# Rotary queries and keys computed feature-major, four heads' halves on the same partitions, and scores on four row tiles

## The chip, the cores and the metric

The kernel runs on one core of a Trainium2 chip. The metric is the device time of one launch in microseconds (us); less is better. TensorE (PE) multiplies matrices, its weight loads are shown apart (PEld); VectorE (DVE), ScalarE (ACT) and GpSimd (POOL) do the elementwise work; DMAs are issued from SyncE's queue (SP) and POOL's.

## The reference, cut to what matters

One layer of a decoder: an input projection, local attention beside a gated linear recurrence (HGRN2), cross-attention on 256 memory tokens, a gated feed-forward block. There are 256 tokens of 1024 features, all float32. The change lies in the attention's queries and keys:

```python
q_a, k_a, v_a, q_b, f_b, i_b, og_b, g_a, g_b = split_cols(xn @ w_in[l])   # q_a, k_a: (256, 1024), 16 heads of 64

def rope(t, pos):            # t: (1, 16 heads, 256 tokens, 64)
    ang = pos * inv_freq     # 32 angles a token, the same for all heads
    t1, t2 = t[..., :32], t[..., 32:]
    return concatenate([t1 * cos(ang) - t2 * sin(ang), t2 * cos(ang) + t1 * sin(ang)])

s = einsum('bhqd,bhkd->bhqk', rope(q), rope(k)) * 64 ** -0.5   # causal; softmax; times v
```

With 256 tokens the block attention is one causal block, so each head needs scores of 256 queries against up to 256 keys.

## The kernel before, in words

**Weights and precision.** Every weight matrix is streamed in units of 128 x 2048 floats (the list `ORDER`, laid out on the host by `lay`). `prep` turns a unit into two halves, `hi` (ACT, line 254, rounded) and `lo` (DVE, line 258, the remainder), each in two pieces of 128 x 1024. There are three buffers for each half, and `nxt` prepares two units ahead of the one in use. The activations are held as `Xh` and `Xl` in `XX`, and a product is the sum of three: hi by hi, hi by lo, lo by hi.

**Two forms of GEMM.** `gemm_t` keeps the tokens' features stationary and streams the weights: 128 tokens on the output's partitions, 512 output features along its columns; one call (two units, 512 features, 256 tokens) has 96 multiplications of 512 columns, in the three lines 310 to 312. `gemm_f` keeps the weights stationary and streams the tokens: 128 output features on the partitions, tokens along the columns; one call is one unit of 256 features and has, for each of two feature blocks, eight pairs: line 331 (the weights' `hi` against `Xh` and `Xl`, 512 columns) and line 332 (the weights' `lo` against `Xh`, 256 columns). The two halves of its 512 columns are added by `halves` (ACT copies one out, line 322, DVE adds the other, line 323). The HGRN2 queries (`ev_q`) and two projections of the cross-attention use `gemm_f` before; the attention's queries and keys use `gemm_t`.

**Queries and keys before.** `ev_rope` takes a block of 128 tokens by 512 features from PSUM: three DVE multiplications by the tables `Ct` and `St` (lines 877 to 879), one POOL addition (line 880), and two ticks later `turn`: four transposes on PE (line 885) and one ACT copy (line 886) into `qT` or `kT`, where the 64 features of a head lie on 64 partitions. There are eight such blocks.

**What sets PE's order.** PE's program order is the order of the code. Beside the GEMMs run generators; `tick`, called after each unit of weights, emits the next step of each. `hgrn` emits small multiplications (lines 642, 705, 715 and 723), `attention` the four quads of heads: `quad(j)` emits the scores of four heads (line 900, into four PSUM banks `as` of the pool `sm`, which has four), three ticks later the transposes of the probabilities (line 931), a tick after those the product with the values (line 945). The order on the other engines is made by the scheduler. A `MATMUL` row of line 900 before has a stationary operand of 64 partitions by 128 columns: two heads, on partitions 0 to 63 and 64 to 127, each in its own tile of rows of the array. An ordinary float32 multiplication (scores, values, lines 642 to 723) gives two MATMUL records in the trace, a transpose or a rounded product one.

Of the kernel before, what the change touches and what calls it, by code (L numbers as in the profile page):

```python
# [11 lines left out]
F32 = mybir.dt.float32  # L12
# [33 lines left out]
def plan():  # L46
    order = []

    def tgroup(name, base):
        return [("T", name, base + c * 512, kh) for c in range(2) for kh in range(2)]  # L50

    order += [("T", "w_in", 4096 + c * 512, kh) for kh in range(2) for c in range(2)]
    order += [("F", "w_in", 3 * 1024 + c * 256) for c in range(4)]
    for base in (5, 2, 0, 1, 6):
        order += tgroup("w_in", base * 1024)
    order += tgroup("w_in", 8 * 1024) + tgroup("w_in", 7 * 1024)
    order += tgroup("w_br_hgrn", 0) + tgroup("w_br_attn", 0)
# [59 lines left out]
def lay(ws):  # L117
    out = np.empty((len(ORDER), 128, 2048), np.float32)
    for i, u in enumerate(ORDER):
        if u[0] == "F":  # L120
            w = ws[u[1]][:, u[2]:u[2] + 256]
            out[i].reshape(128, 8, 256)[...] = w.reshape(8, 128, 256).transpose(1, 0, 2)
        elif u[0] == "T":
            w = ws[u[1]][u[3] * 512:(u[3] + 1) * 512, u[2]:u[2] + 512]
            if i < 3:
# [32 lines left out]
def bc(ap, n, axis):  # L158
    shape = list(ap.shape)
    shape.insert(axis, n)  # L160
    return ap.unsqueeze(axis).to_broadcast(shape)


def build(tc, A, out):
    nc = tc.nc
    V, SC, G, PE, SY = nc.vector, nc.scalar, nc.gpsimd, nc.tensor, nc.sync
    with ExitStack() as ctx:
# [29 lines left out]
        def bank(name, shape=(128, 512)):  # L197
            return sm.tile(list(shape), F32, name=name, tag="sm")
# [233 lines left out]
            part_x(k)  # L432


        Ct = cp.tile([128, 2, 64], F32, name="Ct")
        St = cp.tile([128, 2, 64], F32, name="St")

        def rope_tables():
            posf = small("posf", [2])
# [43 lines left out]
            tc.keep_in_program_order(SC.activation(m, r, AF.Sin))  # L483
            tc.keep_in_program_order(SC.activation(mh, t, AF.Sin))
            for i in range(2):
                rs = r_x[:, i:i + 1]
                for c in range(2):
                    G.tensor_scalar(Ct[:, i, c * 32:(c + 1) * 32], mh[:, i], rs, None, op0=ALU.mult)
                G.tensor_scalar(St[:, i, 0:32], m[:, i], rs, -1.0, op0=ALU.mult, op1=ALU.mult)
                G.tensor_scalar(St[:, i, 32:64], m[:, i], rs, None, op0=ALU.mult)  # L490

        rt = rope_tables()
        region = tc.manual_schedule(engines={mybir.EngineType.Pool})
# [372 lines left out]


        qx = big("B6", "qx", (128, 3072))
        qT = qx[:, 0:2048].rearrange("p (a b) -> p a b", a=8)
        kT = big("B11", "kT")  # L870

        def ev_rope(dst, c):
            def ev(t, ps):
                a = t2("ra")
                b = t2b("rb_")
                p3, a3, b3 = (z.rearrange("p (h d) -> p h d", d=64) for z in (ps, a, b))
                V.tensor_tensor(a3, p3, bc(Ct[:, t], 8, 1), op=ALU.mult)
                V.tensor_tensor(b3[:, :, 0:32], p3[:, :, 32:64], bc(St[:, t, 0:32], 8, 1), op=ALU.mult)
                V.tensor_tensor(b3[:, :, 32:64], p3[:, :, 0:32], bc(St[:, t, 32:64], 8, 1), op=ALU.mult)
                G.tensor_tensor(a, a, b, op=ALU.add)  # L880

                def turn():
# [7 lines left out]
        for c in range(2):  # L890
            gemm_t(X, ev_rope(qT, c))
        rows = (slice(0, 64), slice(64, 128))

        def quad(j):
            sc = []
            for hp in (2 * j, 2 * j + 1):
                ss = [bank("as", (128, 384)) for _ in range(2)]
                for q, o in ((slice(0, 128), slice(0, 128)), (slice(128, 256), slice(128, 384))):
                    for r, ps in zip(rows, ss):
                        PE.matmul(ps[:, o], qT[r, hp, q], kT[r, hp, 0:q.stop], start=True, stop=True)  # L900
                sc.append(ss)
            parts = ((0, 128), (128, 384))
            pr = []
            for ss in sc:
# [55 lines left out]
        oah = big("B12", "oah", dt=F32R)  # L960
        oal = big("B10", "oal", dt=F32R)
        ag = attention()
        gemm_t(X, ev_rope(kT, 0))
        start(ag)
        gemm_t(X, ev_rope(kT, 1))

        def ev_og(c):
            def ev(t, ps):
# [744 lines left out]
```

## Time and profile before

| | before |
|---|---|
| median of 3 runs (lowest, highest) | 593.89 us (593.01, 594.14) |
| profiled execution: its time, its span | 593.53 us, 591.4 us |
| PE busy | 584.3 us, 99% of the span |
| DVE, ACT, POOL busy | 448.0, 388.8, 119.5 us |
| granted TensorE clock, mean | 0.998 |

The span runs from the first to the last instruction of the program; the time has 2.1 us around it. Matrix instructions are pipelined, so a row's duration is longer than what it adds to PE's time; what it adds is read from the start of one piece to the start of the next.

### The profile page before, as it was taken

The numbers are of one execution on the slowest core, as the hardware profiler recorded it, in microseconds if no ns is written. First come the engines' busy times: TensorE is split into PE (matmuls) and PEld (weight loads), VectorE is DVE, ScalarE is ACT, GpSimd is POOL, SyncE is SP. The second block draws the span as 40 slices with busy tenths as digits, with TensorE's granted clock in tenths as the row PEclk, the third lists the DMA queues.
The fourth block names the chain that finished last, engine by engine and source line by source line (L and its number), as shares of the span: only waits on it lengthen the run. The fifth ranks groups of instructions, "written<-read, shape, count | busy, mean of one in ns | idle before, by whom it ended". The sixth has DMA issues, their size and how long they took to land.

```text
span 591.4 us, 8803 instructions
## 1 busy us (share of the span) xinstructions
PE 584.3 (99%) x3374; PEld 487.7 (82%) x3374; DVE 448.0 (76%) x630; ACT 388.8 (66%) x629; POOL 119.5 (20%) x135
## 2 busy tenths in 40 slices
PE   9999999999999999999999999999999999999995
PEld 7888888888888888888888888888888888888884
DVE  6598967778747784748968785987888887777943
ACT  7795645454767575658548677776858676776743
POOL 2897300222301530003202332200000000000002
PEclk9999999999999999999999999999999999999999
DMA  9877987489999899989986895666979969797601
GB/s 339 345 284 273 285 339 284 157 274 311 310 293 377 265 267 286 322 363 304 325 284 173 262 311 180 170 244 240 377 275 303 402 184 424 199 404 203 237 0 71
DMA packets 22585, 161.90 MB, mean 274 GB/s; under 512 B 2832, under 2 KB 3472, under 8 KB 5392
## 3 DMA queue, kind: packets, MB, share of 16 engines
q1 hardware_dynamic: 18368, 135.35, 58.1%
q0 software_dynamic: 3456, 25.17, 22.1%
q10 hardware_dynamic: 720, 0.84, 0.4%
q8 instruction: 26, 0.43, 0.3%
q14 instruction: 15, 0.12, 0.1%
HBM read 160.29 MB, written 34.60 MB: 330 GB/s over the span
## 4 chain that ended last, share of the span: by engine, by line
PE 99%; DVE 0%; ACT 0%; DVEq 0%; issue 0%; ACTq 0%
PE pst L310 13%; PE pst L312 12%; PE pst L311 12%; PE pqA L1129 11%; PE psf L331 8%; PE pqF L1129 6%; PE psf L332 4%; PE acc L310 3%; PE acc L312 3%; PE acc L311 3%; PE pqB L1129 3%; PE psg L588 1%; PE pso L311 1%; PE pso L310 1%; PE pso L312 1%; PE as L900 1%
## 5 line engine op out<-in xcount | busy, mean ns | idle before, releaser
L258 DVE TENSOR_TENSOR lo<-raw,hi 128x1024 fp32r<-128x1024 f32 (+1 forms) x126 | 158.1, 1274 | 48.9 <-ACT hi L254 48.5
L254 ACT ACTIVATE hi<-raw 128x1024 fp32r<-128x1024 f32 (+1 forms) x126 | 126.2, 1027 | 68.0 <-PE pst L312 37.6
L310 PE MATMUL pst<-hi,XX 128*128 128x512 f32 x224 | 89.0, 398 | 0.0
L312 PE MATMUL pst<-hi,XX 128*128 128x512 f32 x224 | 87.3, 390 | 0.0
L311 PE MATMUL pst<-lo,XX 128*128 128x512 f32 x224 | 87.3, 390 | 0.0
L310 PEld LDWEIGHTS pst<-hi,XX 128*128 128x128 f32 x224 | 42.1, 188 | 9.2 <-issue 0.7
L312 PEld LDWEIGHTS pst<-hi,XX 128*128 128x128 f32 x224 | 42.1, 188 | 9.0
L311 PEld LDWEIGHTS pst<-lo,XX 128*128 128x128 f32 x224 | 42.1, 188 | 8.2
L1368 DVE TENSOR_TENSOR lo<-raw,hi 128x2048 fp32r<-128x2048 f32 (+1 forms) x19 | 37.0, 1951 | 10.6 <-ACT hi L1360 10.5
L1360 ACT ACTIVATE hi<-raw 128x1024 fp32r<-128x1024 f32 x32 | 32.0, 1051 | 7.3 <-PE acc L312 5.3
L1368 DVE TENSOR_TENSOR lo<-rawx,hi 128x2048 fp32r<-128x2048 f32 x12 | 27.5, 2288 | 7.5 <-ACT hi L1360 7.5
L1399 POOL DMA_DIRECT2D b<-t x4 | 3.5, 885 | 123.4 <-DVE fu L1462 88.2
L1360 ACT ACTIVATE hi<-rawx 128x1024 fp32r<-128x1024 f32 x24 | 24.1, 1051 | 4.7 <-DMA rawx<-w 1.7
L1129 PE MATMUL pqA<-hi,SS 128*128 128x512 f32 x80 | 26.4, 391 | 0.0
L310 PE MATMUL acc<-hi,hids 128*128 128x512 f32 x62 | 24.4, 394 | 0.0
L312 PE MATMUL acc<-hi,hids 128*128 128x512 f32 x62 | 24.2, 390 | 0.0
L311 PE MATMUL acc<-lo,hids 128*128 128x512 f32 x62 | 24.1, 389 | 0.0
L331 PE MATMUL psf<-XX,hi 128*128 128x512 f32 x64 | 22.9, 401 | 0.0
L331 PE MATMUL psf<-H,hi 128*128 128x512 f32 x64 | 22.8, 400 | 0.0
L331 PE MATMUL psf<-M,hi 128*128 128x512 f32 x64 | 22.7, 398 | 0.0
L1368 DVE TENSOR_TENSOR lo<-b,hi 128x2048 fp32r<-128x2048 f32 x7 | 16.0, 2290 | 5.9 <-ACT hi L1360 5.9
L1368 DVE TENSOR_TENSOR px<-raw,px 128x2048 fp32r<-128x2048 f32 x8 | 18.3, 2284 | 2.1 <-ACT px L1360 2.1
(471 smaller groups left out, 1486.4 us busy)
## 6 DMA issues: line engine op xcount, KB each, us to landing
raw<-w SPq DMA_DIRECT2D x74, 1024.0 KB, 7.6
t<-w POOLq DMA_DIRECT2D x16, 1024.0 KB, 13.0
raw<-t SPq DMA_DIRECT2D x12, 1024.0 KB, 7.4
rawx<-w SPq DMA_DIRECT2D x10, 1024.0 KB, 7.9
b<-w SPq DMA_DIRECT2D x6, 1024.0 KB, 8.4
b<-w POOLq DMA_DIRECT2D x4, 1024.0 KB, 8.5
rawx<-t SPq DMA_DIRECT2D x4, 1024.0 KB, 6.9
b<-t POOLq DMA_DIRECT2D x4, 1024.0 KB, 8.6
```

What stands on the lines that cost most here:

```text
L254: SC.activation(hi[:, a], raw[:, a], AF.Copy)
L258: V.tensor_tensor(lo[:, a], raw[:, a], hi[:, a].bitcast(F32), op=ALU.subtract)
L310: PE.matmul(ps, xh, h, start=first, stop=False)
L311: PE.matmul(ps, xh, l, start=False, stop=False)
L312: PE.matmul(ps, xl, h, start=False, stop=last)
L331: PE.matmul(ps, w[0][:, k, a], X2[:, :, k], start=k == 0, stop=False)
L332: PE.matmul(ps[:, 0], w[1][:, k, a], X2[:, 0, k], start=False, stop=k == 7)
L588: PE.matmul(pss[c][t], z[:, k, t * 128:(t + 1) * 128], ws[c][0][:, k], start=z is Xh and k == 0, stop=False)
L900: PE.matmul(ps[:, o], qT[r, hp, q], kT[r, hp, 0:q.stop], start=True, stop=True)
L1129: PE.matmul(ps, x[k], z[:, k], start=first and k == 0 and i == 0, stop=k == 3 and i == 2, skip_group_check=not first)
L1360: pin(SC.activation(hi[:, a], raw[:, a], AF.Copy))
L1368: pin(V.tensor_tensor(lo[:, a], raw[:, a], hi[:, a].bitcast(F32), op=ALU.subtract))
```

## The change

The queries' and keys' projections go from `gemm_t` to `gemm_f`. Their weight units are laid out so that one unit of 256 features holds the lower 32 features of four heads in its first 128 columns and the upper 32 of the same four in its last 128 (the kind "R"). So a call leaves two blocks of 128 x 256 tokens, the lower and the upper halves of four heads on the same partitions, 32 a head, and the rotation works between the two blocks on equal partitions. It is DVE's two multiplications of 128 x 512 (by cosines, by sines) and POOL's two of 128 x 256, which write `qT` and `kT` directly; the transposes of `turn` and their copies are gone. The tables are made as `CS` (each token's 32 cosines and sines four times over, 128 wide) and turned once by four transposes (`angles`) into `turnsF`, in a buffer (B12) that the attention's output takes later. The scores of four heads now come from four tiles of 32 rows, one for each head, in two accumulating steps (lower and upper half) into the same four banks.

```diff
-    for base in (5, 2, 0, 1, 6):
+    for base in (5, 2):
         order += tgroup("w_in", base * 1024)
+    order += [("R", "w_in", base * 1024 + c * 256) for base in (0, 1) for c in range(4)]
+    order += tgroup("w_in", 6 * 1024)
...
+        elif u[0] == "R":
+            w = ws[u[1]][:, u[2]:u[2] + 256].reshape(8, 128, 4, 2, HD // 2).transpose(1, 0, 3, 2, 4)
+            out[i].reshape(128, 8, 256)[...] = w.reshape(128, 8, 256)
...
-        def ev_rope(dst, c):
-            def ev(t, ps):
-                a = t2("ra")
-                b = t2b("rb_")
-                p3, a3, b3 = (z.rearrange("p (h d) -> p h d", d=64) for z in (ps, a, b))
-                V.tensor_tensor(a3, p3, bc(Ct[:, t], 8, 1), op=ALU.mult)
-                V.tensor_tensor(b3[:, :, 0:32], p3[:, :, 32:64], bc(St[:, t, 0:32], 8, 1), op=ALU.mult)
-                V.tensor_tensor(b3[:, :, 32:64], p3[:, :, 0:32], bc(St[:, t, 32:64], 8, 1), op=ALU.mult)
-                G.tensor_tensor(a, a, b, op=ALU.add)
-
-                def turn():
-                    bk = bank("rT", (128, 4, 128))
-                    for j in range(4):
-                        PE.transpose(bk[:, j], a[:, j * 128:(j + 1) * 128], ident)
-                    SC.activation(dst[:, 4 * c:4 * c + 4, t * 128:(t + 1) * 128], bk, AF.Copy)
-                later.append(lambda: later.append(turn))
+        def angles():
+            b = bank("cs", (128, 2, 2, 128))
+            for c in range(2):
+                for i in range(2):
+                    PE.transpose(b[:, c, i], CS[:, c, i].rearrange("p n f -> p (n f)"), ident)
+            SC.activation(turnsF, b.rearrange("p c i t -> p c (i t)"), AF.Copy)
+
+        def ev_rope(dst, j):
+            z = t2("rz", (128, 2, 256))
+
+            def ev(m, ps):
+                halves(z[:, m], ps)
+                if m == 0:
+                    return
+                a, b = t2("ra", (128, 2, 256)), t2b("rb_", (128, 2, 256))
+                V.tensor_tensor(a, z, bc(turnsF[:, 0], 2, 1), op=ALU.mult)
+                V.tensor_tensor(b, z, bc(turnsF[:, 1], 2, 1), op=ALU.mult)
+                G.tensor_tensor(dst[:, j, 0], a[:, 0], b[:, 1], op=ALU.subtract)
+                G.tensor_tensor(dst[:, j, 1], a[:, 1], b[:, 0], op=ALU.add)
             return ev
...
-            for hp in (2 * j, 2 * j + 1):
-                ss = [bank("as", (128, 384)) for _ in range(2)]
-                for q, o in ((slice(0, 128), slice(0, 128)), (slice(128, 256), slice(128, 384))):
-                    for r, ps in zip(rows, ss):
-                        PE.matmul(ps[:, o], qT[r, hp, q], kT[r, hp, 0:q.stop], start=True, stop=True)
+            ss = [bank("as", (128, 384)) for _ in range(4)]
+            for q, o in ((slice(0, 128), slice(0, 128)), (slice(128, 256), slice(128, 384))):
+                for w in range(2):
+                    for r, ps in zip(quads, ss):
+                        PE.matmul(ps[:, o], qT[r, j, w, q], kT[r, j, w, 0:q.stop], start=w == 0, stop=w == 1)
```

Three places show what moves. On PE, in the queries' projection, the rows around one group of transposes (`rT`, two blocks of four) that stands before HGRN2's products `lv`; first before, then the same place of the change (line numbers are shifted by a few).

```order
L311 MATMUL pst<-lo,XX 128x512
L312 MATMUL pst<-hi,XX 128x512
L885 MATMUL rT<-cst,ra 128x128 x8
L705 MATMUL lv<-QK 32x32 x32
L310 MATMUL pst<-hi,XX 128x512
L311 MATMUL pst<-lo,XX 128x512
```

```order
L336 MATMUL psf<-XX,hi 128x512
L337 MATMUL psf<-XX,lo 128x256
L708 MATMUL lv<-QK 32x32 x32
L336 MATMUL psf<-XX,hi 128x512
L337 MATMUL psf<-XX,lo 128x256
```

The eight transposes are gone, and so are three other groups of eight; the products around them are pairs of 512 and 256 columns in place of triples of 512. On PE at the end of the keys' projection, the first quad's scores, before and after:

```order
L311 MATMUL pst<-lo,XX 128x512
L312 MATMUL pst<-hi,XX 128x512
L900 MATMUL as<-kT,qx 128x128 x2
L900 MATMUL as<-kT,qx 128x256 x2
L900 MATMUL as<-kT,qx 128x128 x2
L900 MATMUL as<-kT,qx 128x256 x2
L310 MATMUL pst<-hi,XX 128x512
```

```order
L336 MATMUL psf<-XX,hi 128x512
L337 MATMUL psf<-XX,lo 128x256
L907 MATMUL as<-kT,qx 128x128 x8
L907 MATMUL as<-kT,qx 128x256 x8
L315 MATMUL pst<-hi,XX 128x512
```

Eight multiplications become sixteen, of the same sizes, each with half the rows. On DVE at the start of the queries' projection, before and after (`lo` is the weights' remainder, QK and ATS belong to HGRN2):

```order
L258 TENSOR_TENSOR lo<-raw,hi 128x1024
L693 COPY_PREDICATED ATS<-lm,lp 128x8x16
L662 TENSOR_TENSOR QK<-QK,Tt 128x128x8
L693 COPY_PREDICATED ATS<-lm,lp 128x8x16
L877 TENSOR_TENSOR ra<-pst,Ct 128x512
L878 TENSOR_TENSOR rb__1267<-pst,St 128x8x32
L879 TENSOR_TENSOR rb__1267<-pst,St 128x8x32
```

```order
L263 TENSOR_TENSOR lo<-raw,hi 128x1024
L328 TENSOR_TENSOR rz<-psf,ku 128x256
L263 TENSOR_TENSOR lo<-raw,hi 128x1024
L328 TENSOR_TENSOR rz<-psf,ku 128x256
L696 COPY_PREDICATED ATS<-lm,lp 128x8x2x8
L890 TENSOR_TENSOR ra<-rz,tables 128x512
L891 TENSOR_TENSOR rb__1227<-rz,tables 128x512
L696 COPY_PREDICATED ATS<-lm,lp 128x8x16
```

The two additions `rz` (which wait for PE's blocks) now stand between the pieces of `lo`, and the multiplications read SBUF in place of PSUM.

## Rows read from the trace of the kernel before

**Rows 1.** The page: span, busy time of the engines, the chain by engine.

```profile
span 591.4 us, 8803 instructions
PE 584.3 (99%) x3374; PEld 487.7 (82%) x3374; DVE 448.0 (76%) x630; ACT 388.8 (66%) x629; POOL 119.5 (20%) x135
...
PE 99%; DVE 0%; ACT 0%; DVEq 0%; issue 0%; ACTq 0%
```

**Rows 2.** All waits of PE: who waited for whom, us, times, longest.

```profile
PE warm L404 <- PEq L1704: 0.8, 1, 0.8
```

**Rows 3.** Timeline of PE around transposes: start us, us, instruction, tiles, shape.

```profile
117.02 0.39 PE L312 MATMUL pst<-hi,XX 128*128 128x512 f32 x1
117.25 1.03 PE L885 MATMUL rT<-cst,ra 128*128 128x128 f32 x8
118.04 0.48 PE L310 MATMUL pst<-hi,XX 128*128 128x512 f32 x1
118.35 0.40 PE L311 MATMUL pst<-lo,XX 128*128 128x512 f32 x1
...
129.02 1.03 PE L885 MATMUL rT<-cst,ra 128*128 128x128 f32 x8
129.99 0.76 PE L705 MATMUL lv<-QK 128*32 128x32 f32 x64
...
157.39 1.95 PE L723 MATMUL lv<-QK 128*128 128x128 f32 x16
159.10 0.48 PE L310 MATMUL pst<-hi,XX 128*128 128x512 f32 x1
```

**Rows 4.** The same: ends of a run of `gemm_f`, of `gemm_t`, four transposes between.

```profile
34.79 0.48 PE L331 MATMUL psf<-XX,hi 128*128 128x512 f32 x1
...
51.82 0.40 PE L310 MATMUL pst<-hi,XX 128*128 128x512 f32 x1
...
239.32 0.66 PE L792 MATMUL hT<-cst,ATS 128*128 128x128 f32 x4
239.73 0.48 PE L310 MATMUL pst<-hi,ob 128*128 128x512 f32 x1
...
256.16 1.47 PE L931 MATMUL aT<-cst,ap 128*128 128x128 f32 x12
```

**Rows 5.** The same: the first quad's scores, and HGRN2's products on column tiles.

```profile
149.12 0.39 PE L312 MATMUL pst<-hi,XX 128*128 128x512 f32 x1
149.44 1.58 PE L900 MATMUL as<-kT,qx 64*128 64x128 f32 x16
150.95 0.50 PE L310 MATMUL pst<-hi,XX 128*128 128x512 f32 x1
...
98.94 0.89 PE L642 MATMUL lp<-QQ,QK 128*32 128x48 f32 x64
99.75 0.50 PE L310 MATMUL pst<-hi,XX 128*128 128x512 f32 x1
```

**Rows 6.** Busy time of the engines in stretches (PE, PEld, DVE, ACT, POOL).

```profile
28.26:51.82 23.56, 23.56 (x139) 20.58 (x138) 21.48 (x30) 19.79 (x37) 21.49 (x29) 1.00 0.73 269
99.75:149.44 49.69, 49.69 (x385) 40.84 (x377) 38.34 (x49) 23.30 (x31) 13.07 (x9) 1.00 0.80 270
```

**Rows 7.** Instructions of single lines: duration ns min/median/max, first and last start.

```profile
L323 DVE TENSOR_TENSOR kx<-psf,ku x16: 402/418/425, 316.2 to 376.9; 128x256 f32<-128x256 f32 x16
L322 ACT ACTIVATE ku<-psf x24: 357/366/390, 34.0 to 375.6; 128x256 f32<-128x256 f32 x24
L670 DVE TENSOR_TENSOR QK<-QK,Tt x1: 684/684/684, 144.1 to 144.1; 128x512 f32<-128x512 f32 x1
L877 DVE TENSOR_TENSOR ra<-pst,Ct x8: 682/691/692, 110.6 to 149.5; 128x512 f32<-128x512 f32 x8
```

**Rows 8.** DVE from 99.75 to 149.44 us, `lo` alone: count, busy us, mean ns.

```profile
L258 DVE TENSOR_TENSOR lo<-raw,hi 128x1024 fp32r<-128x1024 f32 x16 | 22.6, 1426 | 8.5 <-ACT hi L254 8.5
```

**Rows 9.** Timeline of DVE: the last piece of a weight unit's `lo`.

```profile
107.96 1.22 DVE L258 TENSOR_TENSOR lo<-raw,hi 128x1024 fp32r<-128x1024 f32 x1
```

More of the change, by code (lines that the diff above doesn't have):

```diff
@@ L432, in build @@
             part_x(k)
-        Ct = cp.tile([128, 2, 64], F32, name="Ct")
-        St = cp.tile([128, 2, 64], F32, name="St")
+        tables = big("B12", "tables", (128, 1024))
+        CS = tables[:, 0:512].rearrange("p (c i n f) -> p c i n f", c=2, i=2, n=4)
+        turnsF = tables[:, 512:1024].rearrange("p (c t) -> p c t", c=2)
         def rope_tables():
@@ L485, in rope_tables @@
             for i in range(2):
[L486 to L490, printed above, removed]
+                for c, z in enumerate((mh, m)):
+                    G.tensor_scalar(CS[:, c, i], bc(z[:, i], 4, 1), r_x[:, i:i + 1], None, op0=ALU.mult)
         rt = rope_tables()
@@ L868, in build @@
         qx = big("B6", "qx", (128, 3072))
-        qT = qx[:, 0:2048].rearrange("p (a b) -> p a b", a=8)
-        kT = big("B11", "kT")
-        def ev_rope(dst, c):
-            def ev(t, ps):
-                a = t2("ra")
-                b = t2b("rb_")
-                p3, a3, b3 = (z.rearrange("p (h d) -> p h d", d=64) for z in (ps, a, b))
-                V.tensor_tensor(a3, p3, bc(Ct[:, t], 8, 1), op=ALU.mult)
-                V.tensor_tensor(b3[:, :, 0:32], p3[:, :, 32:64], bc(St[:, t, 0:32], 8, 1), op=ALU.mult)
-                V.tensor_tensor(b3[:, :, 32:64], p3[:, :, 0:32], bc(St[:, t, 32:64], 8, 1), op=ALU.mult)
-                G.tensor_tensor(a, a, b, op=ALU.add)
-                def turn():
-                    bk = bank("rT", (128, 4, 128))
-                    for j in range(4):
-                        PE.transpose(bk[:, j], a[:, j * 128:(j + 1) * 128], ident)
-                    SC.activation(dst[:, 4 * c:4 * c + 4, t * 128:(t + 1) * 128], bk, AF.Copy)
-                later.append(lambda: later.append(turn))
-            return ev
@@ L890, in build @@
-        for c in range(2):
-            gemm_t(X, ev_rope(qT, c))
+        qT = qx[:, 0:2048].rearrange("p (j w t) -> p j w t", j=4, w=2)
+        kT = big("B11", "kT", (128, 4, 2, 256))
+        def angles():
[4 more added lines that the diff above has]
+            SC.activation(turnsF, b.rearrange("p c i t -> p c (i t)"), AF.Copy)
@@ L892, in build @@
+        angles()
+        for c in range(4):
+            gemm_f(XX, ev_rope(qT, c))
         rows = (slice(0, 64), slice(64, 128))
         def quad(j):
-            sc = []
-            for hp in (2 * j, 2 * j + 1):
-                ss = [bank("as", (128, 384)) for _ in range(2)]
-                for q, o in ((slice(0, 128), slice(0, 128)), (slice(128, 256), slice(128, 384))):
-                    for r, ps in zip(rows, ss):
-                        PE.matmul(ps[:, o], qT[r, hp, q], kT[r, hp, 0:q.stop], start=True, stop=True)
-                sc.append(ss)
+            ss = [bank("as", (128, 384)) for _ in range(4)]
[3 more added lines that the diff above has]
+                        PE.matmul(ps[:, o], qT[r, j, w, q], kT[r, j, w, 0:q.stop], start=w == 0, stop=w == 1)
+            sc = (ss[0:2], ss[2:4])
@@ L962, in build @@
         ag = attention()
-        gemm_t(X, ev_rope(kT, 0))
-        start(ag)
-        gemm_t(X, ev_rope(kT, 1))
+        for c in range(4):
+            if c == 2:
+                start(ag)
+            gemm_f(XX, ev_rope(kT, c))
         def ev_og(c):
```

## The prediction

> **What bounds the kernel now.** I read the page first: PE is busy for 99% of the span and the chain that ended last lies on PE for 99% of it [rows 1]. A busy PE need not be a limit, since it may be waiting inside its rows, so the waits come next: over the whole span PE waits once, 0.8 us before the warm-up [rows 2]. So the time is the length of PE's stream plus a short head and tail. What a change adds to or takes from that stream it adds to or takes from the time, as long as the other engines keep feeding it; and work taken from DVE, ACT or POOL alone is worth nothing. I therefore price the change in PE's timeline, always from the start of one piece to the start of the next, because the durations of pipelined rows overlap.
>
> **Transposes removed.** A group of eight goes from 117.25 to 118.04, 0.79 us, and the product behind it needs 0.31 us to its successor (118.04 to 118.35) where two products in a steady run lie 0.23 us apart (117.02 to 117.25): 0.87 us in all [rows 3]. Before HGRN2's column tiles the group takes 0.97 us (129.02 to 129.99), but then about 0.09 us of it is the change of tiles, which stays: a change to tiles without transposes takes 0.32 us from the last product (149.12 to 149.44) where 0.23 is normal [rows 3, 5]. That is 0.88. There are four such groups, two to each projection: 4 x 0.88 = **-3.5 us**.
>
> **Transposes added.** `angles` has four, once. Four transposes take 0.41 us (239.32 to 239.73) [rows 4], and the restart behind them 0.08 as above: **+0.5 us**. They need `CS`, which POOL makes where it made `Ct` and `St`, by four instructions in place of eight, some 40 us before; nobody waits for it.
>
> **The GEMM in its other form.** Both stream the same columns: 96 x 512 a call of `gemm_t`, twice a projection, against 64 pairs of 512 + 256. The rows tell what the shape costs. From 34.79 to 51.82 lie 48 pairs: 17.03 us, 0.3548 a pair. From 239.73 to 256.16 lie 72 products of 512 columns: 16.43 us, 0.2282 each, both runs with their restart [rows 4]. Two projections are 128 pairs, 45.4 us, in place of 192 products, 43.8 us: **+1.6 us**. So the projection itself gets dearer, since each weight block is loaded for 768 columns in two instructions, the second of them short; only the transposes pay for it.
>
> **Scores.** Before, a quad has 16 records (8 multiplications, two records each) and takes 1.51 us (149.44 to 150.95) [rows 5]. Its records stand for 8 x 128 + 8 x 256 = 3072 columns. A float32 record of 128 x 128 without tiles costs 1.71 / 16 = 0.107 us (157.39 to 159.10) [rows 3], so these 3072 columns one after another would cost 24 x 0.107 = 2.6 us; the two tiles of 64 rows run side by side. After, a quad has 32 records and 6144 columns, half the rows in each: 5.1 us if one after another, 2.6 us if two run side by side, 1.3 us if four do. Nothing here shows four row tiles. The nearest row is the one with four column tiles: 64 records of 48 columns in 0.81 us (98.94 to 99.75), 0.0127 each, where one alone would need 48/128 x 0.107 = 0.040 [rows 5]; more than three run side by side, with the start and the end counted in. I take four: a quad stays at 1.51 us, **0**. The bounds: nothing lower, since the columns divided by the tiles stay the same, and above, two at a time, 2.6 in place of 1.3 us in four quads, +5.2 us.
>
> A rule of the Trainium skill speaks against the scores: "TensorE: Matmul & The Clock Gate", section LDWEIGHTS, says that a load's time depends on its columns and not on its rows, so a load of 32 rows is as long as one of 64, and there are twice as many. By the rule alone, with two loads at a time, the sum would be that of the third rival below; the same page (Part 3, The mechanism) lets loads overlap where their row groups differ, which by itself gives my zero. No run here shows four.
>
> **Sum.** -3.5 + 0.5 + 1.6 + 0 = **-1.4 us**. The profiled execution took 593.53 us, so 592.1; the median before is 593.89, 0.36 above it, which makes **592.5 us** for the median, 0.24% less.
>
> **What must stay hidden.** DVE. A block of 256 features by 256 tokens (a unit of weights, some 5.6 us of PE) cost it 0.69 + 2 x 0.42 = 1.5 us; now it is two additions `rz` of 0.42 and two products of 0.68 (the row of 128 x 512 in SBUF), 2.2 us [rows 7]. Over eight units that is +5.5 us. In the stretch of the projections DVE is busy for 38.3 of 49.7 us; it becomes 43.8 of some 48.2, 91% [rows 6]. That this can be fed is shown by the HGRN2 queries, the same `gemm_f` with a heavier eviction: DVE is busy 21.5 of 23.6 us there, 91%, POOL 91% and ACT 84% as well, and PE waits nowhere [rows 2, 6]. ACT loses eight copies of the turned blocks and gets sixteen of 0.37 us [rows 7], far from full. What queues behind the new waits: `rz` waits for PE's block and the copy `ku`, and stands between the two pieces of `lo` on DVE's queue, as `ku` stands between the pieces of `hi` on ACT's. A `lo` that ended at 109.2 us belongs to a unit that PE starts at 118.04, 8.9 us later [rows 3, 9]. The second piece now moves behind the second block's eviction, half a unit or 2.8 us later; 6 us of cover remain. If the cover went, PE would wait on line 332 or 331 for `lo`.
>
> PSUM: the four score banks are the whole pool `sm`; before, the same four were taken in two steps within 1.5 us. The bank that `angles` takes is one more turn of the pool, beside work that is long read.
>
> **The rivals.**
> 1. *Two row tiles at a time.* For it: the trace shows two and no more for rows. Against it: four column tiles. Price +5.2 us, so -1.4 + 5.2 = +3.8: 597.7 us. It is the one on the other side; it turns the sign as soon as a quad's scores take more than 1.51 + 1.4/4 = 1.86 us.
> 2. *DVE falls behind.* For it: `lo` already takes 1.43 us on average against 1.22 alone (16 of them, 22.6 us, so 3.1 us of stretching beside POOL's additions) [rows 8, 9], and the two products now read SBUF only, as POOL does. If the stretching doubles, DVE has 47 of 48 us to do, and the order on its queue makes PE wait at some units; I price it at 2 us, between nothing and the 5.5 us that DVE gets in all. Then +0.6: 594.5 us.
> 3. *Loads of weights bound the scores.* With two of them side by side, 32 loads in 16 steps of 0.107 us are 1.7 us, in place of 1.3: +0.4 a quad, +1.6 in all. Then +0.2: 594.1 us. Against it: 16 loads of 64 rows are not seen to limit anything now.
> 4. *More is gained.* The restarts around the groups may be worth more than I see, or the pairs may run without the 0.1 us of their restart: -2.5, 591.4 us.
>
> **Chances.** Forecast (-0.9 to -2.0 us): 62%. Rival 1: 10%, rival 2: 12%, rival 3: 10%, rival 4: 6%. A measurement of this kernel tells some 0.2%, 1.2 us, from no change; my -1.4 lies close to that. Of the forecast's 62% I count two thirds, 41%, as faster and 21% as the same; rival 4 is faster; rival 3 the same; rival 2 half the same, half slower; rival 1 slower. Faster 0.47, same 0.36, slower 0.17. The range: up to 595.5 it holds the forecast and rivals 2 and 3, and leaves out rival 1 (10%) and the worst of rival 2; down to 591.5 it leaves out most of rival 4. The forecast's own range is 591.9 to 593.0.
>
> **What would show it.** In the profile of the changed kernel: no `rT`; four `cs` transposes in 0.4 to 0.5 us; 128 pairs at 0.353 to 0.357 us, so 45.2 to 45.7 us for both projections without the small work between; each quad's scores, 32 records, in 1.5 to 1.6 us, with groups of four starting some nanoseconds apart (right), or over 2.5 us (rival 1), or 1.8 to 2.0 (rival 3); no wait of PE on DVE or ACT between 100 and 160 us (rival 2 would show waits at the first product of a unit or at a `lo`). DVE should be busy about 43 us in that stretch. The prediction is wrong above all if the row tiles do not run four abreast, or if `lo` comes late.

## The result, and the profile after

The changed kernel takes **597.1 us** (median of 4 runs, 596.8 to 598.45) where the kernel before takes 593.5 beside it: a ratio of 1.0065, 95% interval 1.0045 to 1.0085. It is slower by 0.65%, 3.6 us; the forecast was 1.4 us faster, and 597.1 lies above the range. The profiled execution took 596.83 us, 3.3 more than the one before. One execution of `e_late` (831.6 us, mean clock 0.663) is left out below.

The page of the changed kernel, its span, its busy time and its chain by engine, answering to [rows 1]:

```profile
span 594.7 us, 9030 instructions
PE 585.1 (98%) x3474; PEld 489.7 (82%) x3474; DVE 453.4 (76%) x638; ACT 390.2 (66%) x638; POOL 121.2 (20%) x139
...
PE 84%; DVE 5%; DMA 4%; ACT 2%; issue 2%; POOL 1%; SPq 0%; DVEq 0%; POOLq 0%; ACTq 0%
```

PE is busy 0.8 us longer, but the span is 3.3 us longer, and the chain leaves PE for 16% of it. All of PE's waits, which were one row before [rows 2]:

```profile
PE pst L315 <- DVE ob L365: 1.9, 1, 1.9
PE warm L409 <- PEq L1712: 0.8, 1, 0.8
PE pst L317 <- DVE ob L365: 0.6, 1, 0.6
```

Two waits are new, both far behind the rotary, in the projection of the output gates, and both end with `ob` on DVE: the split of a transposed HGRN2 output block (`hT`), which frees the PSUM bank that the next product needs. Where the forecast looked, PE's timeline is as it should be. The four new transposes, the first quad's scores, and the place behind HGRN2's products that stood at 159.10 us [rows 3, 5]:

```profile
99.57 0.66 PE L879 MATMUL cs<-cst,tables 128*128 128x128 f32 x4
99.98 0.48 PE L336 MATMUL psf<-XX,hi 128*128 128x512 f32 x1
...
148.54 1.59 PE L907 MATMUL as<-kT,qx 32*128 32x128 f32 x32
150.06 0.50 PE L315 MATMUL pst<-hi,XX 128*128 128x512 f32 x1
...
157.34 0.48 PE L315 MATMUL pst<-hi,XX 128*128 128x512 f32 x1
```

The stretch began at 99.57 where it began at 99.75 before, and 157.34 stands against 159.10, so the new form gains 1.76 - 0.18 = 1.6 us. PE keeps this lead up to the first wait:

```profile
221.43 0.60 PE L795 MATMUL hT<-cst,ATS 128*128 128x128 f32 x4
223.94 0.64 PE L315 MATMUL pst<-hi,XX 128*128 128x512 f32 x1 [1.91 <-DVE ob L365]
224.38 0.63 PE L316 MATMUL pst<-lo,XX 128*128 128x512 f32 x1
...
248.94 0.39 PE L316 MATMUL pst<-lo,ob 128*128 128x512 f32 x1
249.88 0.50 PE L317 MATMUL pst<-hi,ob 128*128 128x512 f32 x1 [0.55 <-DVE ob L365]
```

The same places before, and the next transposes of `ap` and the last ones after:

```profile
223.12 0.60 PE L792 MATMUL hT<-cst,ATS 128*128 128x128 f32 x4
223.48 0.48 PE L310 MATMUL pst<-hi,XX 128*128 128x512 f32 x1
...
229.06 1.47 PE L931 MATMUL aT<-cst,ap 128*128 128x128 f32 x12
```

```profile
231.08 1.47 PE L938 MATMUL aT<-cst,ap 128*128 128x128 f32 x12
...
259.43 1.47 PE L938 MATMUL aT<-cst,ap 128*128 128x128 f32 x12
```

The products behind the wait are slow, 0.42 us from start to start. The busy times of these stretches say why (the number behind the five engines is the granted clock, then the DMA share); the first row is the rotary's stretch, to be held against [rows 6]:

```profile
99.57:148.54 48.97, 48.97 (x428) 42.07 (x420) 41.54 (x57) 25.84 (x42) 16.54 (x16) 1.00 0.80 282
215.50:221.40 5.90, 5.90 (x29) 4.89 (x28) 4.07 (x12) 4.73 (x11) 3.52 (x4) 1.00 0.73 247
221.40:223.90 2.50, 0.63 (x5) 0.36 (x3) 2.50 (x5) 1.60 (x4) 1.44 (x2) 1.00 1.05 216
223.90:231.10 7.20, 7.16 (x25) 5.74 (x26) 4.13 (x5) 2.75 (x5) 0.00 (x0) 0.76 1.01 234
231.10:239.80 8.70, 8.70 (x57) 7.05 (x55) 3.33 (x4) 6.25 (x11) 0.00 (x0) 1.00 1.02 314
```

The mean clock over the 7.2 us behind the wait is 0.76: PE was at the lower of its levels, 1.2 GHz in place of 2.4, for a part of them. The 24 products up to the next transposes of `ap` take 7.15 us, 5.58 before. So the account is: 1.7 us ahead at 221.4 (221.43 against 223.12 before); 2.2 us of standstill and 1.5 us at the low clock put PE 2.0 us behind at 231.1; the 72 products from 241.8 on, with the second wait, take 17.66 us where 16.43 were taken before [rows 4], +1.2, so 3.3 us behind at 259.4, which is the difference of the two profiled executions. The low clock is not part of every execution: 7.2 us at 0.76 lower the mean over the span by 0.003, to 0.995 in the profiled one, and two of the other three, with 0.998 and 0.999, took 597.4 and 596.8 us all the same. No trace of those is kept, so what they lost in its place is not known.

**Why PE had to wait.** The timeline of DVE around the third quad, with the first row maximum of the softmax, and of ACT at the end; first before:

```profile
208.63 1.23 DVE L258 TENSOR_TENSOR lo<-raw,hi 128x1024 fp32r<-128x1024 f32 x1 [1.00 <-ACT hi L254]
209.78 0.68 DVE L357 TENSOR_TENSOR oal<-ao,oah 128x512 fp32r<-128x512 f32 x1
210.38 0.28 DVE L910 CUSTOM_DVE_ANT_0 ap<-as,cst 128x128 f32<-128x128 f32 x1
...
218.48 1.23 DVE L258 TENSOR_TENSOR lo<-raw,hi 128x1024 fp32r<-128x1024 f32 x1 [0.43 <-ACT hi L254]
219.62 0.48 DVE L360 SCALAR_TENSOR_TENSOR ob<-hT,gv,ob 128x256 fp32r<-128x256 f32 x1
220.02 1.22 DVE L258 TENSOR_TENSOR lo<-raw,hi 128x1024 fp32r<-128x1024 f32 x1
221.15 0.68 DVE L785 TENSOR_TENSOR ATS<-ATS,hr 128x512 f32<-128x512 f32 x1
...
220.14 0.47 ACT L359 ACTIVATE ob<-hT,gv 128x256 fp32r<-128x256 f32 x1 [0.38 <-DVE ob L360]
220.60 0.69 ACT L988 ACTIVATE tat<-pst,r_half 128x512 f32<-128x512 f32 x1
```

and after:

```profile
209.98 0.69 DVE L362 TENSOR_TENSOR oal<-ao,oah 128x512 fp32r<-128x512 f32 x1
210.58 1.22 DVE L263 TENSOR_TENSOR lo<-raw,hi 128x1024 fp32r<-128x1024 f32 x1
211.71 0.29 DVE L917 CUSTOM_DVE_ANT_0 ap<-as,cst 128x128 f32<-128x128 f32 x1
...
221.18 0.69 DVE L788 TENSOR_TENSOR ATS<-ATS,hr 128x512 f32<-128x512 f32 x1 [1.22 <-POOL hr L784]
221.78 0.48 DVE L365 SCALAR_TENSOR_TENSOR ob<-hT,gv,ob 128x256 fp32r<-128x256 f32 x1
222.18 1.22 DVE L263 TENSOR_TENSOR lo<-raw,hi 128x1024 fp32r<-128x1024 f32 x1
223.31 0.48 DVE L365 SCALAR_TENSOR_TENSOR ob<-hT,gv,ob 128x256 fp32r<-128x256 f32 x1
...
222.30 0.47 ACT L364 ACTIVATE ob<-hT,gv 128x256 fp32r<-128x256 f32 x1 [2.04 <-DVE ob L365]
222.67 1.26 ACT L996 ACTIVATE tat<-pst,r_half 128x512 f32<-128x512 f32 x2
```

The scores ended at 209.82 before and at 208.11 after, 1.7 us earlier. Yet the first row maximum comes 1.3 us later, because a `lo` now stands ahead of it; and the first `ob` comes 2.2 us later, behind the scaling of `sg` (`ATS<-ATS,hr`), which waits for a chain that begins with `hon` on ACT (the copy of HGRN2's products `ho` out of PSUM; `sg` is its gated output). Before, that `hon` (213.66) ran between four and four exps; after, it runs behind all eight (216.76). ACT's half of the next split waits for DVE's, and the gates' eviction `tat` stands behind it, so `tat` is 2.1 us late too (222.67 against 220.60). For the last block, `ob` stands behind the whole fourth softmax (249.35) where it stood in its middle (242.16).

DVE was late already when the third quad began. The chain that ended last leaves PE at 148.5 us, passes through two weight transfers, and runs from the second of them, shown here with the `hi` that it releases, over ACT, DVE and POOL to the first wait:

```profile
166.23 14.24 DMA raw<-w
180.49 1.07 ACT hi L259
```

Before, this `hi` started at 179.92, waiting for its weights as well, so PE's lead does not reach it. At the second quad, too, a `lo` now stands ahead of the row maxima (183.33; before behind them, 185.04), and from there on DVE is 1.3 us late (`hss` at 194.15 against 192.86). What the 0.57 us of the transfer and what the order is worth there, no run separates.

One thing more moved, the PSUM banks. In the program the product behind the second transposes waits for ACT before (the bank of `tat`) and for DVE after (the bank of the first `hT` block):

```
L310 MATMUL pst<-hi,XX 128x512 [waits Activation_49]
```

```
L315 MATMUL pst<-hi,XX 128x512 [waits DVE_49,PE_49]
```

Before, `tat` was done at 221.29 and the product began at 223.48, 2.2 us of room. PE 1.7 us earlier and `tat` 2.1 us later use this up and would by themselves make a wait of 1.6 us; the exchanged bank, free only when the second `ob` ends at 223.79, adds the rest of the 2.2. Nobody wrote these orders: the change moves them, on engines that the scheduler fills.

### The profile page after: what moved, and what is told of

The parts are those of the page before. It is cut to its first block, busy times and chain, and to the rows that moved or that the text cites. A ratio compares the mean times of both kernels' runs of the same rounds, so it can differ in the third digit from the quotient of the medians.

```text
span 594.7 us, 9030 instructions
## 1 busy us (share of the span) xinstructions
PE 585.1 (98%) x3474; PEld 489.7 (82%) x3474; DVE 453.4 (76%) x638; ACT 390.2 (66%) x638; POOL 121.2 (20%) x139
## 4 chain that ended last, share of the span: by engine, by line
PE 84%; DVE 5%; DMA 4%; ACT 2%; issue 2%; POOL 1%; SPq 0%; DVEq 0%; POOLq 0%; ACTq 0%
PE psf L336 13%; PE pqA L1137 11%; PE pst L315 7%; PE pst L317 6%; PE pst L316 6%; PE psf L337 6%; PE pqF L1137 6%; PE acc L315 3%; PE acc L317 3%; PE acc L316 3%; PE pqB L1137 3%; DVE lo L263 3%; DMA raw<-w 2%; ACT ap L924 2%; DMA t<-w 2%
## 5 line engine op out<-in xcount | busy, mean ns | idle before, releaser
L263 DVE TENSOR_TENSOR lo<-raw,hi 128x1024 fp32r<-128x1024 f32 (+1 forms) x126 | 154.6, 1243 | 47.8 <-ACT hi L259 47.3
L336 PE MATMUL psf<-XX,hi 128*128 128x512 f32 x192 | 68.6, 402 | 0.0
L315 PE MATMUL pst<-hi,XX 128*128 128x512 f32 x160 | 64.3, 402 | 1.9 <-DVE ob L365 1.9
L316 PE MATMUL pst<-lo,XX 128*128 128x512 f32 x160 | 63.1, 394 | 0.0
L317 PE MATMUL pst<-hi,XX 128*128 128x512 f32 x160 | 63.0, 394 | 0.0
L337 PE MATMUL psf<-XX,lo 128*128 128x256 f32 x192 | 54.0, 281 | 0.0
L336 PEld LDWEIGHTS psf<-XX,hi 128*128 128x128 f32 x192 | 36.1, 188 | 8.8
L315 PEld LDWEIGHTS pst<-hi,XX 128*128 128x128 f32 x160 | 30.4, 190 | 8.9 <-issue 2.8
L337 PEld LDWEIGHTS psf<-XX,lo 128*128 128x128 f32 x192 | 36.4, 189 | 0.0
L317 PEld LDWEIGHTS pst<-hi,XX 128*128 128x128 f32 x160 | 30.5, 191 | 6.5
L316 PEld LDWEIGHTS pst<-lo,XX 128*128 128x128 f32 x160 | 30.5, 190 | 5.9
```

The lines of the kernel that those rows point to most:

```text
L263: V.tensor_tensor(lo[:, a], raw[:, a], hi[:, a].bitcast(F32), op=ALU.subtract)
L315: PE.matmul(ps, xh, h, start=first, stop=False)
L316: PE.matmul(ps, xh, l, start=False, stop=False)
L317: PE.matmul(ps, xl, h, start=False, stop=last)
L336: PE.matmul(ps, w[0][:, k, a], X2[:, :, k], start=k == 0, stop=False)
L337: PE.matmul(ps[:, 0], w[1][:, k, a], X2[:, 0, k], start=False, stop=k == 7)
```

## The experiments

**The theories.** *Order*: the new order on ACT and DVE behind the scores makes PE, which arrives earlier, wait; the low clock is a consequence. *Rotary*: the new form itself costs the time (DVE's added work, the weight loads), wherever PE stands still.

| kernel | median us | ratio to before, 95% interval | PE's standstills in its profile |
|---|---|---|---|
| changed kernel | 597.1 | 1.0045 to 1.0085 | 221.8: 2.2; 248.9: 0.9 |
| `e_late` (before, three instructions held back) | 597.5 | 1.0042 to 1.0073 | 247.5: 1.0; 248.8: 1.4 |
| `e_defer` | 597.0 | 1.0042 to 1.0070 | 221.9: 3.7 |
| `e_defer_one` | 599.45 | 1.0082 to 1.0110 | 191.9: 1.0; 222.9: 4.0; 252.0: 0.9 |
| `e_pairs` (holds the edit of `e_defer` too) | 597.15 | 1.0036 to 1.0078 | 223.3: 2.9 |
| `e_half` (half of the scores) | 592.7 | 0.9975 to 0.9996 | 220: 0.6; 259 to 288: 2.6 |
| `e_ho_first` | 594.2 | 0.9997 to 1.0018 | 289.2: 1.3 |
| `b_ho_first` (before, same move) | 595.8 | 1.0023 to 1.0051 | 282.2: 0.6; 291.4: 1.3 |
| `e_noturn` (before, no transposes) | 590.6 | 0.9936 to 0.9963 | 286.3: 1.1 |
| `ho_two` | 597.1 | 1.0051 to 1.0077 | 221.6: 2.6; 290.6: 1.0 |
| `defer2` | 594.1 | 1.0003 to 1.0027 | 222.1: 1.1; 289.5: 0.8 |
| `fill` | 595.6 | 1.0023 to 1.0048 | 247.5: 0.9 |
| `twice` (before, scores doubled) | 599.1 | 1.0076 to 1.0107 | none |

The standstills are from start to start of neighbouring rows on PE, in us; two products in a steady run lie 0.23 apart. At the second wait the two products behind it are slow to start as well, which makes the 1.2 us that PE loses there.

### `e_late`: the order of the changed kernel in the kernel before

```diff
-                    SC.activation(on, ps, AF.Copy)
+                    with tc.issue_after(marks["e", 2]) if (g, t) == (1, 1) else nullcontext():
+                        SC.activation(on, ps, AF.Copy)
...
+                        if b == 0:
+                            then.enter_context(tc.issue_after(scaled_sg))
+                        elif b == 3:
+                            then.enter_context(tc.issue_after(marks["e", 3]))
+                            then.enter_context(tc.issue_after(marks["n", 3]))
                         split(ps[:, j], obh[:, h], obl[:, h], gv[:, V_HG + h:V_HG + h + 1])
...
```

> The kernel before, rotary and scores as they were, with three instructions held back to where the changed kernel has them: `hon` behind the last exp of the third quad on ScalarE, `ob` of the first transposed block behind the scaling of `sg`, and `ob` of the last block behind the last exp and the last normalise of the fourth quad on VectorE. Order theory: the two stalls appear in the old rotary kernel, with the low clock behind the first; the changed kernel lost 3.6 + 1.3 us between 217 and 259 us, so 593.5 + 4.9 = 598.4 us, range 596.5 to 599. Rotary theory: no stall, 593 to 594 us.

Three runs took 596.1, 597.5 and 598.0 us. The waits of PE in the first:

```profile
PE pst L312 <- DVE ob L360: 1.0, 1, 1.0
PE warm L404 <- PEq L1713: 0.8, 1, 0.8
PE pst L310 <- ACT ob L359: 0.5, 1, 0.5
```

With the old rotary the held-back instructions cost some 3.4 us (0.58%; 2.6 in this profiled execution), but only the second standstill is there, in two pieces. The first does not test the theory: `ob` came 2.4 us later (222.02), yet the scheduler put `tat` ahead of it on ACT (220.93), so the bank was free. The first stall is thus left to the kernels below.

### `e_defer`, `e_defer_one`, `defer2`: the second pair's softmax later in the code

```diff
...
+            soft(sc[0])
+            if j < 2:
+                soft(sc[1])
+            else:
+                behind_all.append(lambda: soft(sc[1]))
```

(`soft` is one pair's softmax, row maxima, exps and normalising; `behind_all` is emptied at the end of `tick`; `e_defer_one` does it for `j == 2` alone; `defer2` leaves the row maxima in place and defers exps and normalising.)

> The changed kernel, with the softmax of the second pair of the third and fourth quads traced at the end of its token tile's step instead of right behind the scores, which puts `hon` back between the four and four exps on ScalarE and `ob` back in the middle of the last softmax on VectorE. Order theory (the loss is the two stalls of PE in front of the products of `og`, at 221.8 and 248.9 us of the changed kernel's trace, and the low clock behind the first): both stalls go, PE keeps the 1.6 us that it was ahead at 217 us, so 593.5 - 1.6 = 591.9 us, range 591.4 to 592.6. Rotary theory (the rotary's new form itself costs the time, by PE or VectorE load, and the stalls only show it elsewhere): no change from the changed kernel, 596.5 to 597.6 us, the gaps wander to other places.

> The changed kernel with the second pair's softmax traced later for the third quad alone. Order theory: the first stall (2.2 us, and 1.56 us of slower products behind it) goes, the second (1.2 us over the last 72 products of `og`) stays: 591.9 + 1.25 = 593.1 us, range 592.6 to 594.0. If the two stalls have one cause in common that sits ahead of both, either both go (591.9) or neither (597).

> The changed kernel with the exps and the normalising of the third and fourth quads' second pair traced at the end of the step, the row maxima left where they are. The earlier deferral moved the row maxima too, and they came behind the first pair's normalising on VectorE (217.7 us). Order theory: `hon` at the place of the kernel before, `ob` of the last block in the middle of the softmax; `ob` of the first block still behind the scaling of `sg` and behind the normalising, so a first stall of 0.5 to 2 us may stay: 592.5 to 595. If the place of `hon` on ScalarE is not what matters, as slow as the changed kernel: 597.

The first two missed. `hon` was back between the exps and the second stall was gone in `e_defer`, but the first became longer, and another row ended it:

```profile
PE pst L317 <- ACT tat L1004: 3.4, 1, 3.4
PE warm L411 <- PEq L1720: 0.8, 1, 0.8
```

The bank is that of `tat` again. The deferred row maxima came behind the first pair's normalising on DVE, so ACT's last four exps ran from 219.79, in front of `ob` and `tat` (224.85). With the maxima left in place (`defer2`) the same wait shrinks to 0.8 us and the time to 594.1: putting back `hon` and the last `ob` is worth 3.0 of the 3.6 us lost. In the profile of `e_defer_one` a third wait stands at 191.9 us, for an earlier `hon`: ACT's order there is that of the changed kernel, but the `hi` ahead of it waited longer for its weights (182.32 us against 180.49), and `hon` comes 1.8 us later. In `defer2` a `lo` still stands ahead of the maxima (first pair's done at 213.43, 211.70 before).

### `e_half`: the order of before with the new rotary

```diff
-                for w in range(2):
-                    for r, ps in zip(quads, ss):
-                        PE.matmul(ps[:, o], qT[r, j, w, q], kT[r, j, w, 0:q.stop], start=w == 0, stop=w == 1)
+                for r, ps in zip(quads, ss):
+                    PE.matmul(ps[:, o], qT[r, j, 0, q], kT[r, j, 0, 0:q.stop], start=True, stop=True)
```

> The changed kernel with only the lower half of each head in the scores: 16 score matmuls a quad in place of 32, the upper halves' 16 left out, so the scores are of half of each head and the output is not the reference's. Built this way, ScalarE and VectorE issue the work of the softmax and of the HGRN output in the order of the kernel before, row for row, with the rotary in its new form. Order theory: no stall at 221.8 and 248.9 us; 593.5 - 1.6 = 591.9 us, less what half of the score matmuls take, at most 4 x 0.6 us: 589.4 to 592.0. Rotary theory (the new rotary itself costs the time): 597.1 less at most 2.4 us, 594.7 to 597.1, with stalls of PE still there.

(The counts there are of records; a multiplication is two.) With eight score multiplications a quad the scheduler's order behind the rotary is that of before again, on ACT and on DVE; ACT's program around `hon`, the changed kernel first, then this one:

```
L924 ACTIVATE ap,asum<-ap,anm 128x256
L778 ACTIVATE hon<-ho 128x512
L780 ACTIVATE hsq<-hon 128x512
```

```
L923 ACTIVATE ap,asum<-ap,anm 128x256
L778 ACTIVATE hon<-ho 128x512
L923 ACTIVATE ap,asum<-ap,anm 128x128
```

The two stalls go but for 0.3 us, with the rotary in its new form: 592.7 us, 4.4 less than the changed kernel. A quad's scores take 0.87 us here and 1.52 there, so at most 4 x 0.65 = 2.6 of these are the scores left out, and at least 1.8 us come back with the order. DVE does not follow PE here either: the third quad's scores begin 2.7 us earlier than before (205.57 against 208.31), its first row maximum at 210.28 against 210.38. That the new form gains time against the kernel before is not shown by this kernel, and it is slower than expected: PE was 3.1 us ahead at the fourth quad's product with the values (259.96 against 263.05) and the profiled execution ends 0.65 us ahead. Its waits show where that went:

```profile
PE mT L1014 <- POOL tat L1009: 1.2, 2, 0.9
PE warm L409 <- PEq L1711: 0.8, 1, 0.8
PE ao L951 <- ACT qx L942: 0.3, 1, 0.3
PE pst L315 <- ACT tat L995: 0.3, 1, 0.3
```

PE now waits at 289 us for POOL's `tat`, behind DVE. In the kernel before the same place had no slack: POOL's first of these two additions ran from 288.64 to 289.93 and PE's transposes of it began at 290.02. DVE is busy for the whole of 276 to 288 us in both, and its `lo` at 252 us came only 0.65 us earlier than before, while the DMA share of 232 to 264 us is 0.98 (1.01 before). That the weight transfers hold this pace is argued from these rows; no run here changes it.

### `e_ho_first`, `b_ho_first`, `ho_two`: the HGRN2 output's step ahead of the quad's

```diff
-        start(ho)
+        bg.insert(0, ho)
```

(`ho_two` puts it first in two of its eight steps.)

> The changed kernel with the HGRN output's step put ahead of the attention quad's in each token tile's step, so `hon` and `ob` are traced in front of the softmax that they stood behind. Order theory: `hon` runs ahead of the third quad's exps and `ob` of the last block ahead of the fourth quad's row maxima; both stalls go and the 1.6 us on PE are kept: 591.9 us, range 591.3 to 593. If it is not `hon` and `ob` but the softmax itself that arrives late (its own users on PE then wait): a new wait at the transposes of `ap`, 593 to 597.

> Control: the kernel before with the same move of the HGRN output's step. It has no stall there to lose: 593.5 us, within 0.5 by either theory. Were it 1.5 us faster, the move would be worth something by itself and the kernel above would say nothing on the stalls.

> The changed kernel with the HGRN output's step put ahead of the quad's in two steps alone: the one that holds `hon` of the last four heads, and the one that holds the last transposed block. Order theory: no stall of PE at 221.8 and 248.9 us, and unlike the kernel that moves all of the HGRN output's steps, no cost of the move at 290 us: PE stays 1.6 us ahead to 264 us. Two outcomes from there: PE sets the end, 591.9 us; or VectorE and the weight loads set the pace from 260 to 293 us (the half-scores kernel came there 3.1 us ahead and kept 0.65 us at the end), 592.7 to 593.5 us. If the stalls come back elsewhere, 594 to 597.

Both new waits go in `e_ho_first`; a wait of 0.9 us for `tat` appears at 290 us, and the time is 594.2, above the expected range. The control was not neutral: the move costs the kernel before 2.2 us, with the same wait for `tat`. So the two belong together: with `hon` and `ob` ahead of the softmax in both kernels, ACT's order is the same in both behind the rotary (DVE's differs in a few places), and the change is worth 594.2 - 595.8 = **-1.6 us** (the intervals leave -0.7 to -2.7); PE is 1.55 us ahead at the fourth quad's product with the values (261.98 against 263.53). `ho_two` missed: the first stall came back (2.3 us, ended by `tat`). The HGRN2 products moved ahead of the third quad's scores there, which so began 1.7 us later (208.27 against 206.58), and its exps ran up to 220.2 us, in front of `ob` and `tat`.

### `fill`: work in the standstill

```diff
                     for t in range(2):
-                        PE.transpose(ps[:, j, t * 128:(t + 1) * 128], sog[:, t, h * 128:(h + 1) * 128], ident)
+                        for _ in range(6 if b == 1 else 1):
+                            PE.transpose(ps[:, j, t * 128:(t + 1) * 128], sog[:, t, h * 128:(h + 1) * 128], ident)
```

> The changed kernel with the four transposes of the second HGRN output block each issued six times into the same place: 20 more, 20 x 0.107 = 2.1 us of work on PE exactly where it stands still for 2.2 us. It parts the loss at that stall into the standstill and the low clock behind it. If the clock falls because PE stands still: the 24 products behind take 5.6 us instead of 7.15 and the time is 597.1 - 1.5 = 595.6 us, range 595.0 to 596.2. If the slow products come from something else (the operands, the weight loads): 597.1, or up to 2 us more if the added work does not fit into the wait.

The two stretches that answer to 221.4 to 231.1 us of the changed kernel:

```profile
221.40:224.10 2.70, 2.70 (x26) 2.60 (x24) 2.70 (x5) 1.67 (x4) 1.57 (x2) 1.00 1.03 209
224.10:229.90 5.80, 5.80 (x28) 4.80 (x28) 4.18 (x5) 2.79 (x5) 0.00 (x0) 1.00 1.04 230
```

Twenty idle transposes more, and the kernel is 1.5 us *faster* than the changed one, as expected: PE is not free any earlier (224.07 against 223.94), but the clock stays at 1.00. The 1.5 us behind the first wait in the profile of the changed kernel are the price of standing still.

### `e_pairs`, `twice`, `e_noturn`: the prices on PE

```diff
+            for two in (slice(0, 2), slice(2, 4)):
                 for q, o in ((slice(0, 128), slice(0, 128)), (slice(128, 256), slice(128, 384))):
                     for w in range(2):
-                        for r, ps in zip(quads, ss):
+                        for r, ps in zip(quads[two], ss[two]):
```

> As the first of these kernels, with each quad's 32 score matmuls written out two row tiles at a time (the first pair's 16, then the second pair's 16) in place of all four abreast. If four row tiles do run abreast, as the groups 7 ns apart suggest, this takes it away: a quad's scores go from 1.5 us to twice that, 2.6 to 3.0 us, and the time goes up by 4 x 1.3 = 5.2 us at most, less what the earlier start of the first softmax gives back: 594 to 597 us. If the array runs two at a time anyway, the time stays that of the first kernel within 0.5 us.

This kernel also defers the softmax as `e_defer` does (not shown in the edit above), so its total stands beside that kernel's 597.0. The first quad of `e_pairs`:

```profile
148.46 2.14 PE L910 MATMUL as<-kT,qx 32*128 32x128 f32 x32
150.53 0.50 PE L317 MATMUL pst<-hi,XX 128*128 128x512 f32 x1
```

2.07 us where the changed kernel takes 1.52 (148.54 to 150.06): 0.55 us more a quad, less than half of the 1.3 expected. The starts of the single records show why: the second pair's first record, of 128 columns, starts 0.56 us into the quad, and the last of the first pair's, of 256 columns, at 1.20. The two pairs overlap, so the edit does not take the four abreast away. From its own start the second pair takes 1.51 us (0.56 to 2.07), as long as all four tiles in the changed kernel, so four tiles do run abreast there; what two at a time would cost is not measured. The total says little, since its four runs are two of 595.8 (mean clock 0.997) and two of 598.5 us (0.993 and 0.994), around the same standstill.

`twice` writes the score multiplication of line 900 a second time below itself:

> The kernel before with each score multiplication issued twice: 16 a quad as in the changed kernel, the rotary and everything else as before. Built this way, ScalarE and VectorE get the order of the changed kernel (`hon` behind all eight exps, `ob` of the last block behind the softmax). On PE a quad's scores go from 1.5 us to about 2.7, 4 x 1.2 = 4.8 us in all, so 598.4 us by that alone, range 597.5 to 598.8, and no stall. Order theory: the standstill at the products that follow the last HGRN output block (2 us or more in the kernel with the three instructions held back) comes on top, and the first one where it shows: 599.5 to 602.5 us.

It took 5.7 us more than before, and its first quad's scores 2.92 us (149.54 to 152.46), 1.41 more: 4 x 1.41 = 5.6. That is all of it; PE waits nowhere, so the surplus that I expected for the order is not there. In its program `hon` stands behind all eight exps, the scaling of `sg` ahead of the first `ob`, and the last `ob` behind the softmax, as in the changed kernel (`lo` stands between the third quad's row maxima, in the changed kernel ahead of them): the number of score multiplications is enough to move them. But counted from the start of the third quad's scores the first `tat` is done after 16.0 us (227.22 - 211.24) and PE needs it after 16.6 (227.82); in the changed kernel it is done after 16.8 (223.36 - 206.58) and PE is there after 15.2. At the second place it is the same: the first half of the last `ob` is done 10.0 us after the start of the fourth quad's scores in both kernels (249.83 - 239.83 and 252.14 - 242.15), and here PE comes 1.4 us later, by its longer scores. So the order costs nothing where PE comes late enough, and `twice` does not show what it costs where PE is on time. That the first stall takes the new order and PE's lead together is worked out from the times above; no kernel with the whole new order and the old rotary's pace shows it.

`e_noturn` copies the rotated rows as they stand:

```diff
-                    for j in range(4):
-                        PE.transpose(bk[:, j], a[:, j * 128:(j + 1) * 128], ident)
-                    SC.activation(dst[:, 4 * c:4 * c + 4, t * 128:(t + 1) * 128], bk, AF.Copy)
+                    SC.activation(dst[:, 4 * c:4 * c + 4, t * 128:(t + 1) * 128],
+                                  a.rearrange("p (j d) -> p j d", j=4), AF.Copy)
```

> The kernel before with the 32 transposes of the rotated rows left out: ScalarE copies the rows to `qT` and `kT` as they stand, so the scores are of wrong operands and the output is not the reference's. What the prediction priced the transposes at, 4 x 0.88 = 3.5 us on PE's queue: 593.5 - 3.5 = 590.0 us, if PE's queue sets the end and ScalarE and VectorE keep their order. If PE would wait at the same places anyway, 592 to 594.

PE is 3.54 us ahead at the fourth quad's product with the values (259.51 against 263.05), the -3.5 of the sum; the time falls by 3.0 us, as PE waits 0.8 us for the same `tat`.

## Why the prediction was wrong

- **Transposes removed, -3.5:** right; 3.54 us on PE in `e_noturn`. **Transposes added, +0.5:** right; 0.41 us and the restart.
- **GEMM in its other form, +1.6, and scores, 0:** right. From start to start the 128 pairs take 46.0 us and the 192 products 44.4. A quad takes 1.52 us (1.51 before), with groups of four abreast, so rivals 1 and 3 are out; that 597.1 lies beside rival 1's 597.7 is chance. PE's stream up to 157 us is 1.6 us shorter, -1.4 was forecast, and the pair of kernels with `ho` first gives -1.6 in time.
- **DVE in the rotary's stretch:** busy 41.5 of 49.0 us, 85% where I had 91%; `rz` 0.415 us, `ra` 0.68, and `lo` stretches less than before (1.29 us on average, 1.43 before [rows 8]). No wait of PE between 100 and 160 us, so rival 2 is out at its place.
- **The step that failed is "What must stay hidden".** It asked whether DVE has time for its added work and whether `lo` stays ahead, between 100 and 160 us only, and took everything behind the scores as it was: "as long as the other engines keep feeding it". The scheduler sees sixteen score multiplications in place of eight and places `lo`, `hon` and `ob` otherwise around the softmax (shown by the programs of `e_half` and `twice`). At the first wait `ob` and `tat` came some 2 us later while PE came 1.7 us earlier, against 2.2 us of room. The price was 2.2 us of standstill, 1.5 us of low clock (`fill`) and 1.2 us at the second wait: 4.9 us, and -1.6 + 4.9 = +3.3, the difference of the profiled executions. For the executions without the low clock the parts of the loss are open. The orders of the two kernels were compared where the rotary is, not at the quads.
- **A second step was too generous:** that a gain on PE's stream passes on to the end. Around 290 us POOL's `tat` ends 0.1 us before PE reads it in the kernel before, so part of any lead is given back there: in `e_noturn` 0.5 us of 3.5 by the medians and 1.0 by the profiled executions, in `e_half` 2.1 and 2.4 us of 3.1. A page with PE busy for 99% and one wait does not show how little slack stands behind it.
- The forecast's sign is thus not refuted for the change, only for the program that came out of it. No version here with all of the scores is faster than the kernel before: the best, `e_ho_first`, lies between 0.03% faster and 0.18% slower, and `defer2` is 0.03 to 0.27% slower. That the order of before, kept exactly with all sixteen multiplications, would bring the whole -1.6 is open; it was not built.

## What to carry to other kernels

Where a scheduler orders some engines, a change is also a change of order elsewhere: compare the order of those engines wherever something that the bounding engine reads is made, not only around the edit. And read for each such place how long before its use the value is there: 2.2 us at the first `tat` and 0.1 us at the second were the room here. A stall of the matmul engine is to be priced with the slow clock that can follow it.

## What the runs showed of the hardware that was not expected

- After standstills of 2.2, 2.9, 3.7 and 4.0 us (changed kernel, `e_pairs`, `e_defer`, `e_defer_one`) the mean granted clock of the next 7 us or so was 0.76 to 0.77. After 1.1 us (`defer2`) it stayed at 1.00, and in the profiled run of `ho_two` after 2.6 us as well; the six runs of that kernel lie between 595.3 (mean clock 0.997) and 598.9 us (0.992). Two of the four executions of the changed kernel, with mean clocks of 0.998 and 0.999, leave no room for it either. So a standstill of some 2 us can bring the low clock and need not.
- Four row tiles of 32 rows run abreast: 32 records of 128 and 256 columns in 1.52 us, with the records of a group starting 7 ns apart. Written two tiles at a time they take 2.07 us, and the trace shows the second pair's records starting beside the first pair's, from 0.56 us on.
